# A hand-written queue order for four engines in the squared-ReLU MLP of a hybrid decoder layer

## The chip, the cores and the metric

The kernel runs on one core of one Trainium2 chip. The core has five engines that work side by side, each on its own queue of instructions: TensorE (PE in the profile, its weight loads PEld), VectorE (DVE), ScalarE (ACT), GpSimd (POOL) and SyncE (SP), which here only issues transfers. Transfers (DMA) from HBM are issued from the queues of SP and of POOL. The metric is the device time of one launch in microseconds, the median of several runs.

## The reference

One decoder layer on 512 tokens of width 1024, all in float32: an RMSNorm, an attention mixer with two head groups, an output projection with residual, then the part that this change touches, the MLP, and a final RMSNorm:

```python
def squared_relu_mlp(h, w_up, w_down):
    return jnp.square(jax.nn.relu(h @ w_up)) @ w_down
...
        h = h + squared_relu_mlp(rmsnorm(h, g_mlp[l]), w_up[l], w_down[l])
    return rmsnorm(h, g_final)
```

`w_up` is 1024 by 4096, `w_down` 4096 by 1024.

## The kernel before

**Precision.** Each float32 operand is split into a high part (rounded to the matmul type fp32r) and a low part, the rest. A product takes three matmuls, high by high, high by low and low by high (`mm3`, L189 to L192). A split is one ScalarE copy (`wh`, `sh`) and one VectorE subtract (`wl`, `sl`, recorded at L118, the helper `sub`). So each weight piece, 128 by 1024 values or 512 KB, costs a transfer, a copy and a subtract before TensorE can use it.

**The MLP in eight groups.** `for e in range(8)` (L1222) takes 512 of the 4096 hidden columns at a time. A group has four up pieces (`f` = 0 to 3, 24 matmuls each). After each, ScalarE does ReLU (L1237) and square (L1238) out of the PSUM bank, and the hidden values are split. The weights of the up pieces come through `ring` (L122 to L180): raw tile `wr` in two buffers, halves split at L164 (high) and L118 (low). Group 0 then does a plain down product: four pieces `wd`, 96 matmuls over four token blocks. Groups 1 to 7 use a scheme with seven products instead of eight (`product`, L1215, 12 matmuls each), in the order A11, S1, S2, A12, S3, S4, A22. Its inputs are sums of hidden blocks, made by `strassen_in` (L1192): R tiles on VectorE, copies at L1197, subtracts at L118. Its weights are sums of down pieces, built by transfers: `more` (L1125, L1127) adds a piece onto a loaded one by an accumulating transfer from POOL's queue, `down_piece` (L1117 to L1123) forms high and low parts mostly by transfers. One raw tile x serves four of the seven weights in turn: it is loaded, split (L1113, L1114), added to, split again, and so on; y serves one.

**PSUM.** Eight banks are handed out in a cycle by `nbank`. `evac` (L1153) adds a bank into the residual `h1`. The products S2, S3, S4 and A22 reuse the banks of earlier ones, so their first matmul waits until `evac` has read what stood there.

**The end.** In group 7, `norm_out` (L1157 to L1182) makes the final norm: a multiply by the gain `gfb` (L1164), a sum of squares on ScalarE (L1167), and for the last part of each token block Ln, Exp, three small VectorE operations, two scalings (L1181) and two transfers out. The last product, A22, is cut into three parts (L1297 to L1303), so that its pieces are finished one by one. The second and the third part share a PSUM bank.

**What sets the order.** TensorE's queue is always written by hand (L75). For the other four engines, the attention part is written by hand up to L1037 (`everything`). From there to the end the framework's scheduler decides in which order their instructions enter each queue. Each engine then runs its own queue strictly in order: an instruction that waits holds back all behind it.

Of the kernel before, what the change touches and what calls it, by code (L numbers as in the profile page):

```python
# [15 lines left out]
P = 128  # L16
D = 1024
S = 512
# [35 lines left out]
def hybrid_layer(tc, x, xT, wp, wfg, cst, gfin, out):  # L54
# [1022 lines left out]
    for tb in range(NT):  # L1077
# [9 lines left out]
        wout_evac(ps, tb, 1)  # L1087
    early = []
# [28 lines left out]
    def down_piece(i):  # L1117

        hi, lo = down_tiles()
        nc.gpsimd.dma_start(hi, wp[i])  # L1120
        nc.scalar.activation(lo, f32(hi), AF.Copy, scale=-1.0)
        nc.gpsimd.dma_start(lo, wp[i], accum_op=ALU.add)
        return [hi], [lo]  # L1123

    def more(r, i):  # L1125

        nc.gpsimd.dma_start(r, wp[i], accum_op=ALU.add)  # L1127

# [28 lines left out]
    def norm_out(tb, c, n, last):  # L1157
# [6 lines left out]
        nc.vector.tensor_tensor(o[:, c:c + n], h, gfb[:, c:c + n], op=ALU.mult)  # L1164
# [27 lines left out]
    def strassen_in(R, sh, sl, p, i):  # L1192
# [13 lines left out]
        sub(nc.vector, R[:, 4], R[:, 3], R[:, 1])  # L1206
        split(S1, 1)
        negsum(5, 0, 4)
        split(S2, 1)
        split(A12, 2)  # L1210
# [10 lines left out]

    for e in range(8):  # L1222
        sh = mp.tile([P, 2, 7, 256], F32R, tag="sh", name=nm("sh"))
        sl = mp.tile([P, 2, 7, 256], F32R, tag="sl", name=nm("sl"))
        ah, al = [t.rearrange("p a b c -> p (a b c)")[:, 0:4 * S].rearrange("p (f t) -> p f t", f=4) for t in (sh, sl)]
        for f in range(4):
            if early:
                w, ps = early.pop(0)
                up_mm(ps, w, range(4, NK))
            else:  # L1230
                w, ps = ring.piece(), nbank()
                up_mm(ps, w, range(NK))
            t = mp.tile([P, S], F32, tag="mt", name=nm("mt"), bufs=2)
            if f % 2 == 0:
                R = mp.tile([P, 8, 256], F32, tag="R", name=nm("R"), bufs=2)
            a = R[:, 2 * (f % 2):2 * (f % 2) + 2, :].rearrange("p a t -> p (a t)")
            nc.scalar.activation(t, ps, AF.Relu)  # L1237
            nc.scalar.activation(a, t, AF.Square)  # L1238
            if e > 0:
                strassen_in(R, sh, sl, f // 2, f % 2)  # L1240
            else:
                nc.scalar.activation(ah[:, f, :], a, AF.Copy)  # L1242
                sub(nc.vector, al[:, f, :], a, f32(ah[:, f, :]))
        w11, w12, w21, w22 = range(next_piece[0], next_piece[0] + 4)
        next_piece[0] += 4
        if e == 0:
            wd = [down_split(raw(i)) for i in (w11, w12, w21, w22)]
            for tb in range(NT):
                pss = [nbank() for _ in range(2)]
                tok = tokens(tb)  # L1250
                for fs in ((0, 1, 2), (3,)) if tb == 0 else ((0, 1, 2, 3),):
                    for half in range(2):
                        for f in fs:
                            mm3(pss[half], ah[:, f, tok], al[:, f, tok], *part(wd[f], 512 * half, 512), f == 0, f == 3)
                for half in range(2):
                    evac(pss[half], tb, 512 * half)
            continue
        pa, pd, pc = [[nbank() for _ in range(2)] for _ in range(3)]
        x, y = raw(w11), raw(w12)
        more(y, w22)  # L1260
        if e == 7:
            gfb = raw()
            nc.sync.dma_start(gfb, gfin.to_broadcast([P, D]))
        product(pa, A11, down_split(x), True, sh, sl)
        for k in range(2):
            evac(pa[k], k, 0)
        more(x, w12)
        product(pd, S1, down_split(x), True, sh, sl)
        for k in range(2):
            evac(pd[k], 2 + k, 512, True)  # L1270
        more(x, w22)
        product(pa, S2, down_split(x), False, sh, sl)
        for k in range(2):
            evac(pa[k], k, 512, True)
        product(pc, A12, down_piece(w21), True, sh, sl)
        for k in range(2):
            evac(pc[k], k, 0)
            if e == 7:
                norm_out(k, 0, 512, False)
# [131 lines left out]
```

## Time and profile before

| | us |
|---|---|
| median of 3 runs | 668.19 |
| lowest, highest | 667.58, 668.45 |
| the profiled execution | 667.41 |
| its span, first to last instruction | 665.6 |
| busy: PE, DVE, ACT, POOL | 637.7, 467.8, 365.5, 173.5 |

The span is shorter than the time by 1.81 us, which lie around it. Busy times are of an engine's instructions, not of its waiting; matmuls overlap, so a busy PE can still hold small gaps. The granted clock is the share of full speed that TensorE had.

### The profile page before, as it was taken

Reading aid. Unit: us, or ns where it says so; the run is one execution under the profiler, and the core shown is the slowest. Engines: PE = TensorE matmul, PEld = TensorE weight load, DVE = VectorE, ACT = ScalarE, POOL = GpSimd, SP = SyncE. Lnnn points to the kernel's source line nnn. Section 1 sums busy time; section 2 is a strip of 40 time slices with the busy share of each in tenths; the row PEclk is TensorE's granted clock in tenths of the full one; section 3 lists DMA queues with packets and bytes.
Section 4 is the critical chain, followed back from the end, with each engine's and each line's share of the span. In section 5 each row is a group of like instructions: output and inputs, shape, how many; then the busy total and the mean of one; then the engine's idle time right before and its main releaser. Section 6 shows DMA issues by size and latency. Waiting matters only on the chain.

```text
span 665.6 us, 9186 instructions
## 1 busy us (share of the span) xinstructions
PE 637.7 (96%) x3075; PEld 521.2 (78%) x3075; DVE 467.8 (70%) x1032; ACT 365.5 (55%) x776; POOL 173.5 (26%) x223
## 2 busy tenths in 40 slices
PE   9999999999999999999969999999999999999993
PEld 7867788878887878888848888788787887877882
DVE  5798887867866789948623575766756767567577
ACT  5435536777867878738612635617347173371633
POOL 0262062655756745200101102012021110101100
PEclk9999999999999999999969999999999999999997
DMA  8723621001122574134962935849569385572803
GB/s 273 235 95 127 213 72 33 2 33 32 33 82 71 127 219 109 53 105 176 284 141 54 245 109 136 248 90 245 151 134 266 80 242 154 130 184 35 187 1 126
DMA packets 28926, 88.74 MB, mean 133 GB/s; under 512 B 4944, under 2 KB 5584, under 8 KB 28880
## 3 DMA queue, kind: packets, MB, share of 16 engines
q1 hardware_dynamic: 20672, 58.76, 26.5%
q0 software_dynamic: 8064, 29.36, 21.6%
q8 instruction: 24, 0.39, 0.2%
q14 instruction: 22, 0.18, 0.1%
q10 hardware_dynamic: 144, 0.04, 0.0%
HBM read 81.83 MB, written 2.10 MB: 126 GB/s over the span
## 4 chain that ended last, share of the span: by engine, by line
PE 45%; DMA 22%; DVE 17%; ACT 9%; issue 5%; SPq 1%; POOL 1%; DVEq 0%; ACTq 0%; POOLq 0%
DMA wr<-wp_d 18%; DVE wl L118 5%; PE acc L190 4%; PE acc L191 4%; PE acc L192 4%; DVE h L1153 4%; PE O L756 4%; PE T L738 4%; PE S L192 3%; PE S L190 3%; PE S L191 3%; ACT wh L164 2%; ACT wh L1113 2%; PE S L710 2%; PE O L190 2%
## 5 line engine op out<-in xcount | busy, mean ns | idle before, releaser
L118 DVE TENSOR_TENSOR wl<-wr,wh 128x512 fp32r<-128x512 f32 (+1 forms) x141 | 123.1, 886 | 99.0 <-ACT wh L164 64.4
L164 ACT ACTIVATE wh<-wr 128x512 fp32r<-128x512 f32 x120 | 72.5, 623 | 61.0 <-DMA wr<-wp_d 26.5
L1113 ACT ACTIVATE wh<-wr 128x1024 fp32r<-128x1024 f32 x39 | 40.3, 1052 | 105.7 <-DMA wr<-wp_d 86.5
L1127 POOL DMA_DIRECT2D wr<-wp_d x28 | 24.5, 879 | 267.0 <-DVE wl L118 194.0
L720 ACT ACTIVATE sp<-sp,st 128x128 f32<-128x128 f32 (+1 forms) x96 | 53.2, 555 | 17.2 <-DVE st L718 16.6
L718 DVE CUSTOM_DVE_ANT_0 sp<-S,c 128x128 f32<-128x128 f32 (+1 forms) x96 | 43.1, 486 | 18.6 <-PE S L711 18.1
L726 POOL TENSOR_SCALAR sp<-sp,st,gt 128x128 f32<-128x128 f32 (+1 forms) x64 | 38.2, 607 | 47.8 <-ACT sp L720 26.9
L118 DVE TENSOR_TENSOR ptl<-T,pth 128x128 fp32r<-128x128 f32 (+1 forms) x96 | 44.3, 483 | 2.9 <-ACT pth L748 2.4
L748 ACT ACTIVATE pth<-T 128x128 fp32r<-128x128 f32 (+1 forms) x96 | 38.4, 426 | 9.8 <-PE T L738 9.2
L190 PE MATMUL S<-wh,sh 128*128 128x512 f32 (+1 forms) x92 | 36.2, 394 | 5.2 <-DVE h L1153 4.1
L738 PE MATMUL T<-c,sp 128*128 128x128 f32 x240 | 38.4, 274 | 2.5 <-DVE st L724 1.3
L118 DVE TENSOR_TENSOR sl<-R,sh 128x256 fp32r<-128x256 f32 (+1 forms) x74 | 37.7, 534 | 2.8 <-ACT sh L1242 1.7
L738 PEld LDWEIGHTS T<-c,sp 128*128 128x128 f32 x240 | 29.6, 140 | 12.4 <-issue 4.5
L1197 ACT ACTIVATE sh<-R 128x256 fp32r<-128x256 f32 (+1 forms) x70 | 33.8, 502 | 8.8 <-DVE R L1201 7.9
L191 PE MATMUL S<-wh,sl 128*128 128x512 f32 (+1 forms) x92 | 36.1, 392 | 0.0
L192 PE MATMUL S<-wl,sh 128*128 128x512 f32 (+1 forms) x92 | 35.9, 391 | 0.0
L190 PE MATMUL S<-uh,wh 128*128 128x512 f32 x88 | 34.4, 391 | 0.0
L191 PE MATMUL S<-uh,wl 128*128 128x512 f32 x88 | 34.3, 390 | 0.0
L192 PE MATMUL S<-ul,wh 128*128 128x512 f32 x88 | 34.3, 389 | 0.0
L190 PE MATMUL acc<-xh,wh 128*128 128x512 f32 x72 | 31.0, 430 | 0.0
L190 PE MATMUL T<-wh,sh 128*128 128x512 f32 x60 | 24.0, 401 | 6.2 <-ACT sh L1242 6.0
L192 PE MATMUL acc<-xl,wh 128*128 128x512 f32 x72 | 28.4, 395 | 0.0
(361 smaller groups left out, 1795.0 us busy)
## 6 DMA issues: line engine op xcount, KB each, us to landing
wr<-wp_d SPq DMA_DIRECT2D x77, 512.0 KB, 4.3
wr<-wp_d POOLq DMA_DIRECT2D x28, 512.0 KB, 5.5
wh<-wp_d POOLq DMA_DIRECT2D x14, 512.0 KB, 6.2
wl<-wp_d POOLq DMA_DIRECT2D x14, 512.0 KB, 9.2
wx<-wp_d SPq DMA_DIRECT2D x10, 512.0 KB, 4.3
xr<-x_d SPq DMA_DIRECT2D x4, 512.0 KB, 7.9
out_d<-wr SPq DMA_DIRECT2D x8, 256.0 KB, 2.2
xr<-xT_d SPq DMA_DIRECT2D x3, 512.0 KB, 6.6
```

The lines of the kernel that those rows point to most:

```text
L118: eng.tensor_tensor(o, a, b, op=ALU.subtract)
L164: high = lambda: nc.scalar.activation(hi, raw[:, c], AF.Copy)
L190: nc.tensor.matmul(ps, lh, rh, start=first, stop=False, **kw)
L191: nc.tensor.matmul(ps, ll, rh, start=False, stop=False, **kw)
L192: nc.tensor.matmul(ps, lh, rl, start=False, stop=last, **kw)
L718: nc.vector.tensor_tensor_reduce(out=self.p[i], in0=self.ps[i], in1=self.bias(i), scale=1.0, scalar=1e35, op0=ALU.add, op1=ALU.min, accum_ ...
L720: nc.scalar.activation(self.p[i], self.p[i], AF.Exp, bias=m, scale=-1.0, accum_out=den)
L726: nc.gpsimd.tensor_scalar(self.p[i], self.p[i], rs, g, op0=ALU.mult, op1=ALU.mult)
L738: nc.tensor.transpose(pt[:, j * P:j * P + P], self.p[i][:, j * P:j * P + P], ident)
L748: nc.scalar.activation(self.blocks(self.th, i), self.pt[i], AF.Copy)
L1113: nc.scalar.activation(hi, r, AF.Copy)
L1197: nc.scalar.activation(sh[:, p, o], r, AF.Copy)
```

## The change

The MLP from L1129 on gets an order of its own for VectorE, ScalarE, GpSimd and SyncE: the program text is rearranged, and a second `manual_schedule` block makes each of the four queues follow it. The set of operations stays the same but for one: the multiply by `gfb` goes from VectorE to GpSimd, except in the last quarter row.

- Up pieces: `up_fetch(g)` issues the load, `up_split(g)` the split, two steps ahead of the matmuls that use the piece, and after a split the load of the piece two further on.
- Group 0: the loads of its four down pieces, then of up pieces 3 and 4, stand first in SP's queue; each down piece is split in the step of its number. x and y of group 1 are loaded after the last up piece of group 0, and x is split between the second and third token block.
- Groups 1 to 7: the weight splits for S1, S3 and S2 stand before the matmuls of f = 1, 2 and 3, that for A22 behind the evacuation of S2, that for the next group's A11 behind the evacuation of A12.
- `hidden` does ReLU, square and the splits. For f = 3 the splits of A12, S3 and S4 are held back (a generator) until the evacuation of A11 is in the queue.
- The last group's `norm_out` calls stand where they stood in the text, and now bind.

```diff
+    first_up = next_piece[0]
...
-    def down_piece(i):
+    def down_whole(i):
         hi, lo = down_tiles()
         nc.gpsimd.dma_start(hi, wp[i])
+        yield [hi], [lo]
         nc.scalar.activation(lo, f32(hi), AF.Copy, scale=-1.0)
         nc.gpsimd.dma_start(lo, wp[i], accum_op=ALU.add)
-        return [hi], [lo]
+        yield
...
+    def up_fetch(g):
+        if g < 32:
+            up_raws[g] = rp.tile([P, 1024], F32, tag="wr", name=nm("wr"), bufs=2)
+            nc.sync.dma_start(up_raws[g], wp[piece_at(g // 4, g % 4)])
+
+    def up_split(g):
+        if not 2 < g < 32:
+            return
+        r, w = up_raws.pop(g), ([], [])
+        for k in range(2):
+            c = slice(512 * k, 512 * k + 512)
+            hi = rp.tile([P, 512], F32R, tag="wh", name=nm("wh"), bufs=6)
+            lo = rp.tile([P, 512], F32R, tag="wl", name=nm("wl"), bufs=6)
+            nc.scalar.activation(hi, r[:, c], AF.Copy)
+            sub(nc.vector, lo, r[:, c], f32(hi))
...
+        up_fetch(g + 2)
+
+    everything = tc.manual_schedule(engines={mybir.EngineType.DVE, mybir.EngineType.Activation, mybir.EngineType.Pool,
+                                               mybir.EngineType.SP})
+    everything.__enter__()
...
-        nc.vector.tensor_tensor(o[:, c:c + n], h, gfb[:, c:c + n], op=ALU.mult)
+        (nc.vector if tb == 3 and last else nc.gpsimd).tensor_tensor(o[:, c:c + n], h, gfb[:, c:c + n], op=ALU.mult)
...
         sub(nc.vector, R[:, 4], R[:, 3], R[:, 1])
+        negsum(5, 0, 4)
         split(S1, 1)
-        negsum(5, 0, 4)
         split(S2, 1)
+        yield
         split(A12, 2)
...
+    def hidden(e, f, ps):
...
+        nc.scalar.activation(t, ps, AF.Relu)
+        nc.scalar.activation(a, t, AF.Square)
+        if e > 0:
+            rest = strassen_in(R, cur["sh"], cur["sl"], f // 2, f % 2)
+            next(rest, None)
+            return rest
...
+    def load_sums(e):
+        X[e], Y[e] = raw(piece_at(e, 4)), raw(piece_at(e, 5))
+
+    def first_sum(e):
+        T[e, 1] = down_split(X[e])
+        more(X[e], piece_at(e, 5))
+        more(Y[e], piece_at(e, 7))
+
+    def next_sum(e, n, i):
+        T[e, n] = down_split(X[e])
+        if i is not None:
+            more(X[e], piece_at(e, i))
+
+    def whole(e, n, i):
+        g = down_whole(piece_at(e, i))
+        T[e, n] = next(g)
+        return g
+
+    downs = [raw(piece_at(0, 4 + i)) for i in range(4)]
+    up_fetch(3)
+    up_fetch(4)
...
     for e in range(8):
...
         for f in range(4):
+            if e == 0:
+                T[0, f] = down_split(downs[f])
+            elif f == 0:
+                if e == 1:
+                    wholes[1, 2] = whole(1, 2, 6)
+                wholes[e, 3] = whole(e, 3, 7)
+            elif f == 1:
+                next_sum(e, 5, 7)
+                next(wholes[e, 2])
+            elif f == 2:
+                T[e, 7] = down_split(Y[e])
+                next(wholes[e, 3])
+            else:
+                next_sum(e, 6, 6)
+            up_split(4 * e + f + 2)
...
+            rest = hidden(e, f, ps)
+            if f < 3:
+                next(rest, None)
         if e == 0:
+            load_sums(1)
             for tb in range(NT):
+                if tb == 2:
+                    first_sum(1)
...
         pa, pd, pc = [[nbank() for _ in range(2)] for _ in range(3)]
+        if e < 7:
+            load_sums(e + 1)
...
+        product(pa, A11, T[e, 1], True, sh, sl)
+        both(pa, 0, 0)
+        next(rest, None)
+        product(pd, S1, T[e, 5], True, sh, sl)
+        both(pd, 2, 512, True)
+        product(pa, S2, T[e, 6], False, sh, sl)
+        both(pa, 0, 512, True)
+        next_sum(e, 4, None)
+        product(pc, A12, T[e, 2], True, sh, sl)
+        both(pc, 0, 0)
+        if e < 7:
+            first_sum(e + 1)
+        else:
+            for k in range(2):
+                norm_out(k, 0, 512, False)
+        product(pa, S3, T[e, 7], False, sh, sl)
+        both(pa, 2, 512, True)
+        if e == 7:
+            for k in range(2):
+                norm_out(2 + k, 512, 512, False)
+        product(pd, S4, T[e, 3], False, sh, sl)
+        both(pd, 0, 512, True)
+        if e < 7:
+            wholes[e + 1, 2] = whole(e + 1, 2, 6)
+            product(pa, A22, T[e, 4], False, sh, sl)
+            both(pa, 2, 0)
+            continue
         for k in range(2):
...
+            norm_out(k, 512, 512, True)
         for k, c, n in ((0, 0, 512), (1, 0, 256), (1, 256, 256)):
...
             evac(pa[k][:, c:c + n], 2 + k, c, n=n)
             norm_out(2 + k, c, n, c + n == 512)
+    everything.__exit__(None, None, None)
```

`both` is `evac` for the two banks of a product, `T` holds the finished weights, `X` and `Y` are the raw tiles x and y by group.

## Rows read from the trace of the kernel before

**Rows 1.** The page's first part: busy microseconds, share of the span and instructions of each engine.

```profile
PE 637.7 (96%) x3075; PEld 521.2 (78%) x3075; DVE 467.8 (70%) x1032; ACT 365.5 (55%) x776; POOL 173.5 (26%) x223
```

**Rows 2.** What TensorE waited for from 300 us on: matmul's tile and line, the releaser; total us, times, longest.

```profile
PE T L190 <- ACT sh L1242: 6.0, 1, 6.0
PE S L190 <- DVE h L1153: 4.1, 1, 4.1
```

**Rows 3.** Busy time by stage: the down product of group 0 with its waits, groups 1 to 6 (from the first up matmul of a group to that of the next), the rest from A22's first matmul on; then a stretch inside the first row. Columns: from:to, length, busy (instructions) of PE, PEld, DVE, ACT and POOL, granted clock, DMA share, GB/s.

```profile
330.56:361.78 31.22, 25.18 (x97) 19.95 (x96) 8.75 (x11) 4.98 (x7) 1.42 (x2) 0.84 0.43 94
361.78:402.65 40.87, 40.87 (x181) 33.80 (x180) 26.37 (x44) 18.77 (x32) 4.89 (x6) 1.00 0.66 168
402.65:444.25 41.60, 41.44 (x181) 33.64 (x180) 27.61 (x46) 20.09 (x33) 6.27 (x8) 1.00 0.70 177
444.25:486.71 42.46, 41.76 (x181) 33.63 (x180) 28.07 (x46) 20.08 (x33) 6.29 (x8) 1.00 0.70 174
486.71:528.26 41.55, 41.42 (x182) 33.63 (x180) 27.99 (x46) 20.08 (x33) 6.29 (x8) 1.00 0.69 177
528.26:571.19 42.93, 41.73 (x181) 33.63 (x180) 27.87 (x46) 20.09 (x33) 6.33 (x8) 1.00 0.67 172
571.19:613.18 41.99, 41.77 (x182) 33.62 (x180) 27.93 (x46) 19.97 (x33) 5.44 (x7) 1.00 0.54 125
651.32:665.60 14.28, 3.77 (x19) 3.03 (x17) 10.28 (x31) 4.91 (x18) 0.00 (x0) 0.73 0.40 147
...
340.90:347.30 6.40, 6.40 (x15) 4.76 (x16) 2.14 (x3) 0.00 (x0) 0.15 (x1) 0.51 0.84 164
```

**Rows 4.** The chain of waits through the gap in group 0: start, us, what.

```profile
324.75 12.80 DMA wr<-wp_d
...
337.57 1.06 ACT wh L1113
...
340.87 0.80 PE T L190
```

**Rows 5.** Group 5 in order of time, ScalarE and TensorE: start, us, instruction, in brackets the idle time before it and its releaser.

```profile
552.11 0.63 ACT L164 ACTIVATE wh<-wr 128x512 fp32r<-128x512 f32 x1 [4.74 <-DMA wr<-wp_d]
552.65 0.58 ACT L1237 ACTIVATE mt<-O 128x512 f32<-128x512 f32 x1
...
555.31 0.51 PE L190 MATMUL S<-wh,sh 128*128 128x512 f32 x1 [0.99 <-ACT sh L1197]
```

**Rows 6.** Single instructions in order of time, for durations: ScalarE, then VectorE.

```profile
307.02 1.14 ACT L164 ACTIVATE wh<-wr 128x512 fp32r<-128x512 f32 x2
...
408.38 2.01 ACT L1113 ACTIVATE wh<-wr 128x1024 fp32r<-128x1024 f32 x2 [2.15 <-DMA wr<-wp_d]
...
635.17 0.60 ACT L1237 ACTIVATE mt<-O 128x512 f32<-128x512 f32 x1 [3.73 <-PE O L192]
635.80 0.63 ACT L1238 ACTIVATE R<-mt 128x512 f32<-128x512 f32 x1
...
636.46 0.42 DVE L118 TENSOR_TENSOR R<-R 128x256 f32<-128x256 f32 x1 [4.57 <-ACT R L1238]
636.92 0.43 DVE L1201 SCALAR_TENSOR_TENSOR R<-R 128x256 f32<-128x256 f32 x1
637.26 1.36 DVE L118 TENSOR_TENSOR sl<-R,sh 128x512 fp32r<-128x512 f32 x3
```

**Rows 7.** Transfers of 512 KB by kind from 362 to 613 us (out<-in, queue, count, KB each, median us from issue to landing), then two single ones, issued at 421.88 (accumulating) and at 458.41 (a load).

```profile
wr<-wp_d SPq DMA_DIRECT2D x32, 512.0 KB, 5.9
wr<-wp_d POOLq DMA_DIRECT2D x22, 512.0 KB, 5.5
wl<-wp_d POOLq DMA_DIRECT2D x12, 512.0 KB, 9.4
...
wr<-wp_d POOLq DMA_DIRECT2D x1, 512.0 KB, 8.3
...
wr<-wp_d SPq DMA_DIRECT2D x1, 512.0 KB, 9.1
```

**Rows 8.** The end, VectorE and ScalarE in order of time.

```profile
650.84 0.75 DVE L1153 SCALAR_TENSOR_TENSOR h<-acc,n2s,h 128x512 f32<-128x512 f32 x1
651.68 0.63 ACT L1167 ACTIVATE jo<-h 128x512 f32<-128x512 f32 x1 [1.32 <-DVE h L1153]
652.44 0.29 ACT L1174 ACTIVATE t<-sso,eb 128x1 f32<-128x1 f32 x1
...
657.09 0.47 DVE L1153 SCALAR_TENSOR_TENSOR h<-S,r2s,h 128x256 f32<-128x256 f32 x1
...
660.26 0.29 ACT L1174 ACTIVATE t<-sso,eb 128x1 f32<-128x1 f32 x1
661.27 1.00 DVE L1181 TENSOR_SCALAR wr<-wr,r,t 128x512 f32<-128x512 f32 x2
```

**Rows 9.** GpSimd's two-input operation: first its group in the list by line and shape (busy us, mean ns), then single instructions of GpSimd and VectorE in order of time.

```profile
L118 POOL TENSOR_TENSOR wl<-wr,wh 128x512 fp32r<-128x512 f32 x18 | 24.5, 1381 | 3.5 <-ACT wh L164 3.4
...
28.54 1.43 POOL L531 TENSOR_TENSOR ck<-ck,r 128x512 f32<-128x512 f32 x1 [7.56 <-DVE r L205]
28.38 2.14 DVE L118 TENSOR_TENSOR wl<-wr,wh 128x512 fp32r<-128x512 f32 x2
31.05 1.28 DVE L118 TENSOR_TENSOR wl<-wx,wh 128x512 fp32r<-128x512 f32 x2
```

More of the change, by code (lines that the diff above doesn't have):

```diff
@@ new lines, in hybrid_layer @@
+    cur, X, Y, T = {}, {}, {}, {}
+    def load_sums(e):
[13 more added lines that the diff above has]
+    downs = [raw(piece_at(0, 4 + i)) for i in range(4)]
@@ L1222, in hybrid_layer @@
+    up_fetch(3)
+    up_fetch(4)
+    wholes = {}
     for e in range(8):
[L1223 to L1225 removed]
+        for n in ("sh", "sl"):
+            cur[n] = mp.tile([P, 2, 7, 256], F32R, tag=n, name=nm(n))
+        sh, sl = cur["sh"], cur["sl"]
         for f in range(4):
[L1227 removed]
+            if e == 0:
[13 more added lines that the diff above has]
+            up_split(4 * e + f + 2)
+            if e == 0 and f < 3:
@@ L1230, in hybrid_layer @@
             else:
[L1231 to L1245, printed above, removed]
+                ps = nbank()
+                up_mm(ps, up_ready.pop(4 * e + f), range(NK))
+            rest = hidden(e, f, ps)
+            if f < 3:
+                next(rest, None)
         if e == 0:
-            wd = [down_split(raw(i)) for i in (w11, w12, w21, w22)]
+            ah, al = cur["a"]
+            load_sums(1)
             for tb in range(NT):
+                if tb == 2:
+                    first_sum(1)
                 pss = [nbank() for _ in range(2)]
@@ L1257, in hybrid_layer, with both @@
             continue
+        def both(banks, tb, c, neg=False):
+            for k in range(2):
+                evac(banks[k], tb + k, c, neg)
         pa, pd, pc = [[nbank() for _ in range(2)] for _ in range(3)]
-        x, y = raw(w11), raw(w12)
-        more(y, w22)
-        if e == 7:
+        if e < 7:
+            load_sums(e + 1)
+        else:
             gfb = raw()
             nc.sync.dma_start(gfb, gfin.to_broadcast([P, D]))
-        product(pa, A11, down_split(x), True, sh, sl)
@@ L1265, in hybrid_layer @@
-        for k in range(2):
[L1266 to L1279, printed above, removed]
@@ L1280, in hybrid_layer @@
-        product(pa, S3, down_split(y), False, sh, sl)
-        for k in range(2):
-            evac(pa[k], 2 + k, 512, True)
-            if e == 7:
-                norm_out(2 + k, 512, 512, False)
-        product(pd, S4, down_piece(w22), False, sh, sl)
-        for k in range(2):
-            evac(pd[k], k, 512, True)
-            if e == 7:
-                norm_out(k, 512, 512, True)
-        more(x, w21)
-        w = down_split(x)
-        if e < 7:
-            product(pa, A22, w, False, sh, sl)
-            for k in range(2):
-                evac(pa[k], 2 + k, 0)
-            continue
+        product(pa, A11, T[e, 1], True, sh, sl)
```

25 lines of the change are left out of this document (22 added, 3 removed).

## Prediction, made before the changed kernel ran

> **What bounds the kernel now.** I began with the busy shares: TensorE is busy for 637.7 of 665.6 us [rows 1], so the kernel is bound by matmuls. What another order can win is time in which TensorE stands still or runs slowly. The list of its waits names two long ones in the MLP, 6.0 us on ScalarE and 4.1 us on VectorE [rows 2]. The table by stage says what they cost [rows 3]. Group 1 takes 40.87 us for its 180 matmuls with TensorE busy throughout: 0.227 us per matmul, the floor. Groups 2 to 6 take 41.60, 42.46, 41.55, 42.93 and 41.99, together 6.18 us over five floors. The down product of group 0 takes 31.22 us for 96 matmuls, whose floor is 96 x 0.227 = 21.8: 9.4 us over. The last 14.28 us hold 3.77 us of matmuls: an end in which a chain of small operations rules.
>
> Then the reasons. In group 0 the chain of waits [rows 4] shows TensorE waiting for ScalarE, whose weight copy (L1113) had waited for a sum of weights of group 1 that took 12.80 us to land. The ReLU of group 0's last up piece stood behind that copy in the queue. So work for the next group held up work needed at once. After the gap the granted clock is 0.51 for 6.40 us, the lower level, 1.2 GHz, and 15 matmuls run at about half speed [rows 3]; this is part of the 9.4. In group 5 it is the same in small: ScalarE idles 4.74 us for the load of an up piece, copies it, and only then does the ReLU, and TensorE then waits 0.99 us for a copy of S1 or S2 [rows 5].
>
> **Durations.** ScalarE: a half up piece 0.52 us (two end 1.14 after the first starts), a down piece 0.96, ReLU to square 0.63, square to the next operation 0.66. VectorE: a 256-wide operation 0.42, one that depends on it 0.46 later, three subtracts in a row 1.36 [rows 6]; an evacuation 0.75 [rows 8].
>
> **Group 0 in the new order.** Per up piece ScalarE has ReLU, square and copy (0.63 + 0.66 + 0.53), the next down piece (0.96) and two up halves (1.04): 3.82 us. From the end of f = 0 the matmuls of f = 1, 2 and 3 need 12 + 12 + 24 matmuls, 10.9 us; three such steps are 11.5, so the last ReLU comes 0.6 us late. Its split takes 0.63 + 0.66 + 0.63 + 0.68 = 2.6, ready 3.2 us after the matmuls of f = 3. TensorE meanwhile has 18 matmuls over f = 0 to 2, 4.1 us: no wait, 0.9 to spare. Up piece 3 is split 3.82 + 0.68 = 4.5 us after f = 0 and wanted at 5.4. Nothing of group 1 stands in front any more: x and y are loaded behind the last up piece. So the whole 9.4 us should go, the slow clock with it.
>
> **Groups 1 to 6.** Here the order must carry itself. The worst step is f = 2: ScalarE still has the chain of f = 1 (up to the S3 copy about 4.9 us: 1.29 to the square's end, 0.91 to the first subtract, 1.3 for three, 0.8 for R6 and R7, 0.52), then two down pieces (1.92) and two halves (1.04): 7.9 us against 5.44 of matmuls. In f = 3 it has 1.6 + 0.96 + 1.04, reaching the last ReLU at 11.5 against 10.9: 0.6 late. S1 is then ready 0.63 + 0.66 + 0.46 + 0.46 + 0.42 = 2.6 after that ReLU's start, some 3.4 us after A11 begins, and is wanted at 18 matmuls, 4.1. The two evacuations of A11 come next on VectorE and end at about 4.8 and 5.4; S2 wants the first bank at 5.4 and the second at 6.1. So about 0.6 us to spare at both places, and no stall: 6.2 us gained. The splits of up pieces, ahead of the ReLU before too, no longer wait, because a load is issued two steps, some 10.5 us, before its split; single loads took 5.9 at the median, 9.1 in a burst [rows 7]. The held-back splits of f = 3 (A12, S3, S4) fall into 8 us of A11, S1 and S2.
>
> **The end.** Here the order written down costs. Let T be the time since A11 of group 7 began (before: 72 matmuls ahead of A22, which began at 651.32 [rows 3], so at 651.32 - 72 x 0.227 = 634.98; S4's first evacuation at 650.84 [rows 8] is T 15.9). VectorE must now finish both last `norm_out` calls before the first evacuation of A22. Each needs its multiply from GpSimd, 1.38 us [rows 9]; four multiplies queue from T 11.7 (when A12 is evacuated) and the two last follow at once: done at 11.7 + 5 x 1.38 = 18.6 and 20.0. Ln to scaling is 1.01 us, squares to Ln 0.76 [rows 8]; the first scaling could start at T 18.6. Whether VectorE may scale while GpSimd multiplies is a price that no row shows for this very operation. From below: no hindrance, then the second pair of scalings runs at T 20.0 to 21.0. From above: the nearest row. A pair of two-input subtracts took 2.14 us while a GpSimd operation of 1.43 us ran, 1.28 without one [rows 9]: VectorE stood until GpSimd was done. Then the first pair starts at 20.0 and the second ends at 22.3. I take this, since the scaling too works from tile to tile in SBUF. A22's first part is then evacuated, and its own `norm_out` (0.77 + 0.76 + 1.01 to the scaling, 0.92 for it, some 3.5 with the evacuation's start) delays the second evacuation to T 25.7; without hindrance 24.4. Before, it began at 657.09, T 22.1 [rows 8]. From there on nothing changes. So the end is 3.6 us longer; with the lower bound 2.3.
>
> The Trainium skill, SBUF — State Buffer, SBUF: two separate sides, says that VectorE and GpSimd share one pair of ports, held exclusively for a whole instruction when VectorE works in a two-port mode or with two SBUF inputs, and it so speaks against moving the multiply. The trace agrees for two inputs (2.14 against 1.28); for the scaling no run here shows it yet. By the rule the sum is the one with 3.6, without it 1.3 us less.
>
> **Sum.** Profiled execution 667.41 - 9.4 - 6.2 + 3.6 = 655.4; the median of the runs is 0.8 above that execution, so 656.2. I say 656.0. A measurement of this kernel can tell about 0.2%, 1.3 us, from no change.
>
> **Rivals.**
> - *Stalls stay in the groups.* The 0.6 us to spare is thin: a load or sum landing a microsecond late (needed 10.5 to 11 us after issue, 8.3 to 9.4 seen [rows 7]) or a ReLU late by more sends the rest to TensorE, 0.5 to 1 us in each of six groups: 3 to 6 us, 659 to 662. For it: the old order lost as much. Against: the lengths above fit.
> - *Group 0 still waits* (the change doesn't do there what it says): the schedule between L1037 and L1129 is still the framework's, and if it puts the start of the new block 2 us late, TensorE waits for f = 3 and may lose its clock again: up to 9 us, 660 to 665.
> - *The x sums set the pace* (the other side). Each group's x is loaded, split and added to three times in a row, at fixed places in the queues. The last sum is issued about 1.2 us after A11 begins; its copy, low half, two evacuations, the next group's low half and one evacuation (1.1 + 1.2 + 1.3 + 1.2 + 0.8 = 5.6) must be done when A22 begins at 16.3. So it must land within 9.5 us. Sums now take 5.5 at the median, 8.3 at worst in these groups, but the low halves, behind others, 9.4 [rows 7]. From 9.5 on, each microsecond costs about one in each of six groups; at 11.7 the gain of 12.0 is eaten, beyond it the kernel is slower than before, 670 at 12.
> - *The end is not longer*: no hindrance, and multiplies shorter than 1.38: 653 to 654.5.
>
> **Chances.** The forecast with its two bounds (654.5 to 658) 0.60; stalls stay 0.17; group 0 waits 0.08; the end not longer 0.05; x sums 0.06, of which 0.05 slower; nothing moves (the gains lost one way or another) 0.04. Faster: 0.60 + 0.17 + 0.08 + 0.05 + 0.01 = 0.91; same 0.04; slower 0.05. The range 653 to 662 holds the first two, nearly all of the fourth and a quarter of the third: about 0.83.
>
> **What the new profile would show.** Right: no TensorE wait in the MLP but the one of its last matmuls; clock 1.00 throughout group 0; groups of 40.9 us; L1164's successor on POOL at about 1.4 us each; the second A22 evacuation 25 to 26 us after A11 of group 7 begins; the list of TensorE's waits with one entry of 6 to 8 us, the last part of A22. Wrong: `sh` or `h` in TensorE's waits for several groups, or ScalarE idle for `wr` at f = 3 or before the A22 weights.

## The result, and the profile after

The changed kernel took 655.93 us at the median of four runs (655.69 to 656.97), the kernel before 667.88 beside it (667.25 to 668.45): a ratio of 0.9824, 95% interval 0.9807 to 0.9841. The profiled execution took 655.86 us with a span of 654.1. The forecast was 656.0.

The busy shares of the changed kernel (us, share of the span, instructions):

```profile
PE 630.2 (96%) x3075; PEld 519.6 (79%) x3075; DVE 470.0 (72%) x1024; ACT 368.5 (56%) x776; POOL 183.9 (28%) x231
```

TensorE lost 7.5 us of busy time [rows 1] although it does the same matmuls. By the stages, 3.4 of it went in group 0's down product (25.18 to 21.79), where matmuls had run at half speed, and 3.8 in groups 2 to 6 (208.1 to 204.3), where the clock was 1.00 before and after: there small gaps between overlapping matmuls had counted as busy. TensorE's list of waits from 310 us to the end has one entry (total, times, longest):

```profile
PE S L190 <- DVE h L1185: 7.8, 1, 7.8
```

It is the last part of A22, in the end. Of the two long entries of before [rows 2] only the first, 6.0 us, is gone. The second, 4.1 us, was this same wait (it ended at 657.62, where A22's last part began), and it has grown to 7.8. The table by stage (us; PE, PEld, DVE, ACT, POOL busy; granted clock, DMA share, GB/s): the down product of group 0, groups 1 to 6, and the end from A22 on.

```profile
330.75:352.54 21.79, 21.79 (x98) 18.02 (x96) 9.31 (x12) 4.75 (x8) 3.07 (x4) 1.00 0.57 159
352.54:393.41 40.87, 40.87 (x182) 33.78 (x181) 28.38 (x45) 20.54 (x33) 6.39 (x8) 1.00 0.65 157
393.41:434.27 40.86, 40.86 (x181) 33.78 (x180) 28.57 (x46) 20.54 (x33) 6.37 (x8) 1.00 0.73 181
434.27:475.14 40.87, 40.87 (x182) 33.78 (x180) 28.58 (x46) 20.43 (x33) 6.37 (x8) 1.00 0.73 181
475.14:516.01 40.87, 40.87 (x182) 33.79 (x181) 28.56 (x46) 20.54 (x33) 6.35 (x8) 1.00 0.71 175
516.01:556.87 40.86, 40.86 (x181) 33.78 (x180) 28.55 (x46) 20.54 (x33) 6.37 (x8) 1.00 0.75 182
556.87:597.74 40.87, 40.87 (x182) 33.78 (x180) 28.57 (x46) 20.43 (x33) 6.36 (x8) 1.00 0.77 197
...
635.87:654.10 18.23, 3.89 (x19) 3.15 (x17) 11.02 (x27) 5.07 (x18) 4.99 (x5) 0.68 0.31 115
```

Set against [rows 3]: group 0's down product 31.22 to 21.79, with the clock at 1.00, is -9.43. Groups 2 to 6 now stand at the floor of 40.87: -6.18. The end, from the start of A11 of group 7 (619.53) to the last instruction, is 34.57 against 665.60 - 634.97 = 30.63: +3.94. The MLP's down product began 0.19 later than before (330.75 against 330.56). The sum is -11.5, and the spans differ by 654.1 - 665.6 = -11.5. Nothing is left over.

The end in order of time, VectorE first, then GpSimd (start, us, instruction; T is the time less 619.53):

```profile
634.36 0.15 DVE L1201 TENSOR_SCALAR eb<-sso 128x1 f32<-128x1 f32 x1 [0.19 <-ACT jo L1199]
...
636.08 0.75 DVE L1185 SCALAR_TENSOR_TENSOR h<-O,n2s,h 128x512 f32<-128x512 f32 x1
637.00 0.64 DVE L1208 SCALAR_TENSOR_TENSOR v<-sso,eb 128x1 f32<-128x1 f32 x1 [0.17 <-ACT jo L1199]
637.75 1.13 DVE L1209 SCALAR_TENSOR_TENSOR t<-r,v 128x1 f32<-128x1 f32 x1
...
639.17 1.00 DVE L1213 TENSOR_SCALAR wr<-wr,r,t 128x512 f32<-128x512 f32 x2
640.09 0.15 DVE L1208 SCALAR_TENSOR_TENSOR v<-sso,eb 128x1 f32<-128x1 f32 x1
640.35 0.22 DVE L1209 SCALAR_TENSOR_TENSOR t<-r,v 128x1 f32<-128x1 f32 x1
...
640.79 1.00 DVE L1213 TENSOR_SCALAR wr<-wr,r,t 128x512 f32<-128x512 f32 x2
641.71 0.74 DVE L1185 SCALAR_TENSOR_TENSOR h<-T,r2s,h 128x512 f32<-128x512 f32 x1
...
645.35 0.48 DVE L1185 SCALAR_TENSOR_TENSOR h<-S,r2s,h 128x256 f32<-128x256 f32 x1
...
631.31 7.55 POOL L1196 TENSOR_TENSOR wr<-h,wr 128x512 f32<-128x512 f32 x6 [10.39 <-DVE h L1185]
```

Six multiplies run back to back on GpSimd until 638.86. While they run, two VectorE operations on a single column, v and t, take 0.64 and 1.13 us; after them the same two take 0.15 and 0.22. At 1.26 us for each multiply the fifth ends at 637.60 and the sixth at 638.86; v ends at 637.64 and t at 638.88. The evacuation at 636.08 and the one-column operation eb at 634.36, which has one input in SBUF, ran beside the multiplies at their usual 0.75 and 0.15. The evacuation of A22's first bank starts at T 22.2, that of the second at T 25.8, where before it started at T 22.1 [rows 8].

### The profile page after: what moved, and what is told of

Read it like the earlier page. It is cut to its first block, busy times and chain, and to the rows that moved or that the text cites. A ratio compares the mean times of both kernels' runs of the same rounds, so it can differ in the third digit from the quotient of the medians.

```text
span 654.1 us, 9165 instructions
## 1 busy us (share of the span) xinstructions
PE 630.2 (96%) x3075; PEld 519.6 (79%) x3075; DVE 470.0 (72%) x1024; ACT 368.5 (56%) x776; POOL 183.9 (28%) x231
## 4 chain that ended last, share of the span: by engine, by line
PE 84%; DVE 9%; DMA 2%; issue 2%; ACT 2%; SPq 0%; POOL 0%; DVEq 0%; ACTq 0%
PE S L192 8%; PE S L190 8%; PE S L191 8%; PE acc L190 6%; PE acc L192 6%; PE acc L191 6%; PE O L190 5%; PE O L192 5%; PE O L191 5%; PE T L192 5%; PE T L190 5%; PE T L191 5%; PE O L756 4%; PE T L738 4%; PE S L710 2%
## 5 line engine op out<-in xcount | busy, mean ns | idle before, releaser
L118 DVE TENSOR_TENSOR wl<-wr,wh 128x512 fp32r<-128x512 f32 (+1 forms) x141 | 120.2, 884 | 22.3 <-ACT wh L1114 11.4
L1129 POOL DMA_DIRECT2D wr<-wp_d x28 | 24.6, 959 | 246.4 <-DVE wl L118 246.4
L118 DVE TENSOR_TENSOR sl<-R,sh 128x256 fp32r<-128x256 f32 (+1 forms) x74 | 39.9, 539 | 60.3 <-ACT sh L1229 52.8
L164 ACT ACTIVATE wh<-wr 128x512 fp32r<-128x512 f32 x62 | 36.3, 622 | 15.3 <-DMA wr<-wp_d 7.1
L1150 ACT ACTIVATE wh<-wr 128x512 fp32r<-128x512 f32 x58 | 32.9, 615 | 0.0
L1262 ACT ACTIVATE mt<-S 128x512 f32<-128x512 f32 x11 | 6.4, 585 | 39.9 <-PE S L192 39.9
```

The source lines that it names most:

```text
L118: eng.tensor_tensor(o, a, b, op=ALU.subtract)
L164: high = lambda: nc.scalar.activation(hi, raw[:, c], AF.Copy)
```

## Experiments

Beside the three groups of runs that follow, the kernel before took 665.97, 667.20 and 665.94 us. Small differences are therefore read from stages of the profiles, not from times on different chips.

### Which part of the change wins what

My theory was that the hand order is the cause of both gains. Four kernels divide it.

**Hand order for group 0 alone.**

```diff
         if e == 0:
...
                 for half in range(2):
                     evac(pss[half], tb, 512 * half)
+            everything.__exit__(None, None, None)
             continue
...
-    everything.__exit__(None, None, None)
```

> The new text, but the hand-written order of the four engines ends after group 0; groups 1 to 7 and the end are ordered by the scheduler again. If the three terms are separate, the 9.4 us of group 0 are gained, the groups keep stalls of some 6 us and the end is as long as before: about 658.5 (667.9 - 9.4). Rival: the rearranged text alone, which the scheduler takes as its priorities, already removes the stalls of the groups: about 652.

Measured: 659.55 us (656.91 to 662.29), ratio 0.9899 (0.9859 to 0.9938). The table by stage: group 0's down product, groups 1 and 2, and the end from A11 of group 7 on.

```profile
330.92:352.71 21.79, 21.79 (x97) 18.02 (x96) 10.83 (x15) 5.95 (x10) 3.21 (x4) 1.00 0.81 246
352.71:396.36 43.65, 41.48 (x182) 33.71 (x180) 27.02 (x44) 19.32 (x33) 6.31 (x8) 1.00 0.78 187
396.36:439.04 42.68, 41.45 (x182) 33.71 (x180) 27.89 (x45) 19.70 (x34) 6.34 (x8) 1.00 0.69 173
...
627.68:657.60 29.92, 19.55 (x91) 16.08 (x89) 21.94 (x49) 11.76 (x33) 9.56 (x8) 0.87 0.19 70
```

Group 0 is cured, the groups stall again (8.0 us over six floors, where the kernel before lost 6.2), and the end is 29.92, shorter than by hand (34.57) by 4.65. The time lies 1 us above the 658.5 expected: the stalls were 1.8 larger than in the kernel before, the end 0.7 shorter.

**Hand order for the groups alone.** The first kernel for this moved only the block's entry. In its trace ScalarE goes through group 0 in the changed kernel's order all the same, so the order seems to be taken from where the block is created, and the run is a repeat of the changed kernel.

```diff
-    everything.__enter__()
...
+            everything.__enter__()
             continue
```

> The other half: the scheduler orders group 0, the hand-written order begins with group 1. If it is the scheduler's queue order that put work of group 1 in front of group 0's last ReLU, the 9.4 us come back: about 665. Rival: the loads of x and y now stand behind group 0's last up piece in the text, and that alone cures it: about 656.

Measured: 655.77 us (655.49 to 656.07), ratio 0.9842 (0.9816 to 0.9867), a second measurement of the change. It decides nothing between the theory and the rival, though the rival's number came out. The next kernel also creates the block there, at the end of group 0's branch:

```diff
-    everything = tc.manual_schedule(engines={mybir.EngineType.DVE, mybir.EngineType.Activation, mybir.EngineType.Pool,
-                                               mybir.EngineType.SP})
-    everything.__enter__()
...
+            everything = tc.manual_schedule(engines={mybir.EngineType.DVE, mybir.EngineType.Activation, mybir.EngineType.Pool,
+                                                       mybir.EngineType.SP})
+            everything.__enter__()
             continue
```

> The scheduler orders group 0 and the hand order opens only at the end of group 0's branch, so groups 1 to 6 and the end are in the hand order. My theory (the scheduler's order puts group 1's work ahead of group 0's last ReLU, and the hand order of group 0 is what takes that away): here nothing of group 1 is in the scheduled stretch, so the scheduler has nothing to put ahead; group 0's down projection then lasts 21.8 us without a long wait, the groups 40.9 each and the time is that of the changed kernel, 655.5 to 656.5. Rival (the scheduler's order is bad for group 0 by itself, whatever is behind it): down of group 0 stays near 31 us and the time is 664 to 666.

Measured: 656.1 us (655.39 to 656.41), ratio 0.9826 (0.9805 to 0.9847). Group 0's down product and group 1, in the order of the scheduler and by hand:

```profile
330.66:352.46 21.80, 21.80 (x98) 18.02 (x96) 6.57 (x9) 2.27 (x4) 0.56 (x1) 1.00 0.16 56
352.46:393.32 40.86, 40.86 (x181) 33.78 (x180) 27.18 (x43) 20.54 (x33) 6.38 (x8) 1.00 0.55 137
```

Group 0 needs no hand order when nothing of group 1 is there to be put in front.

**The rearranged text, no hand order at all.**

```diff
-    everything = tc.manual_schedule(engines={mybir.EngineType.DVE, mybir.EngineType.Activation, mybir.EngineType.Pool,
-                                               mybir.EngineType.SP})
-    everything.__enter__()
...
-    everything.__exit__(None, None, None)
```

> The text of the changed kernel, its statements in their new order, but no hand-written block in the MLP: the scheduler orders the four engines, with the text's order as its priorities. My theory (the scheduler's model of times, not the order of the statements, makes it issue work of the next group ahead): group 0's wait returns in part or whole, the groups stall by 1 to 2 us each as in the kernel before, and the time is 663 to 668. Rival A (the order of the text was the cure): 655.5 to 656.5, groups 40.9. Rival B (the text cures group 0 alone, the groups keep stalling): 659 to 661.

Measured: 656.78 us (654.86 to 658.24), ratio 0.9836 (0.9807 to 0.9864), a span of 655.7. My theory fell: group 0's wait did not return. Rival B had the mechanism and missed the time by 2.2 us at least; the end by the scheduler is 4.6 us shorter than by hand, which its sum did not have. Stages: group 0's down product, groups 1, 2 and 5, the end.

```profile
330.50:352.29 21.79, 21.79 (x98) 18.02 (x96) 6.88 (x10) 3.67 (x6) 1.42 (x2) 1.00 0.46 116
352.29:393.16 40.87, 40.87 (x182) 33.79 (x181) 27.20 (x44) 19.07 (x32) 6.33 (x8) 1.00 0.75 191
393.16:435.97 42.81, 41.60 (x182) 33.63 (x180) 27.89 (x45) 19.90 (x33) 6.33 (x8) 1.00 0.69 172
...
520.32:563.11 42.79, 41.85 (x182) 33.62 (x180) 27.89 (x45) 20.46 (x34) 6.41 (x8) 1.00 0.69 172
...
625.77:655.70 29.93, 19.55 (x91) 16.08 (x89) 21.94 (x49) 11.76 (x33) 9.56 (x8) 0.86 0.19 70
```

ScalarE at the last ReLU of group 0, then in group 5 the copy of an up piece and the last ReLU:

```profile
327.97 0.63 ACT L1150 ACTIVATE wh<-wr 128x512 fp32r<-128x512 f32 x1 [0.42 <-PE O L192]
330.69 0.60 ACT L1258 ACTIVATE mt<-O 128x512 f32<-128x512 f32 x1 [2.10 <-PE O L192]
...
540.37 0.63 ACT L1150 ACTIVATE wh<-wr 128x512 fp32r<-128x512 f32 x1 [4.77 <-DMA wr<-wp_d]
...
544.69 0.58 ACT L1258 ACTIVATE mt<-O 128x512 f32<-128x512 f32 x1
```

Here ScalarE idles 2.10 us and does the ReLU at 330.69; before, in the same place, it had taken up the copy that waited until 337.57 [rows 4].

In the groups the pattern is the one that the prediction read in [rows 5]: in group 5 ScalarE stands idle 4.77 us for the load of an up piece and only then goes on to its ReLUs. The last ReLU of groups 2 to 5 begins 2.60, 1.92, 2.01 and 2.58 us after the group's A11 (542.11 in group 5), in the kernel before 1.25, 2.13, 1.21 and 2.60. By hand it begins 0.96 after it, and no up piece is waited for there. That a late ReLU costs TensorE time is tested by itself below; whether the earlier loads or the place of the copies makes the ReLU early was not tried.

From A11 of group 7 on, this kernel's span differs from the changed one by +6.24 (625.77 against 619.53: the stalls of the groups, less 0.25 that its down product began earlier) and -4.64 (the end): 654.1 + 6.24 - 4.64 = 655.7. So in these two executions the hand order as such is worth 1.6 us of span: it wins the groups and pays most of it back in the end. The two stages differ by far more than 1.6, but as a time the 1.6 is not shown: the text-only kernel's four runs lie between 654.86 and 658.24, and the intervals of the two ratios overlap. The 9.4 us of group 0 came with the rearranged text; which of its changes turned the scheduler's order there was not tried.

### What group 0's loss was

One fault put back into the hand order: a copy that must wait for a sum, ahead of the last ReLU. For that x and y of group 1 are loaded earlier, and the copy of x itself comes ahead of the ReLU as well.

```diff
                 T[0, f] = down_split(downs[f])
+                if f == 2:
+                    load_sums(1)
+                elif f == 3:
+                    first_sum(1)
+                    next_sum(1, 5, 7)
...
             elif f == 1:
-                next_sum(e, 5, 7)
+                if e > 1:
+                    next_sum(e, 5, 7)
...
-            load_sums(1)
...
-                if tb == 2:
-                    first_sum(1)
```

> The changed kernel's hand order with one fault put back: x and y of group 1 are loaded in the step of f = 2 of group 0, and in the step of f = 3, ahead of the last ReLU, ScalarE copies x, a sum is added to it, and the copy of that sum stands ahead of the ReLU too, as in the kernel before. My theory (one copy that waits for a sum, ahead of a ReLU that is ready, is the whole of group 0's loss): x lands at 331 to 333, its sum 8 to 9 us later, the ReLU starts at 341 to 343 instead of 331, TensorE waits 8 to 11 us, its clock falls for a while, the down product of group 0 takes 32 to 36 us against 21.8, groups 1 to 6 stay at 40.9, and the time is 666 to 670. Rival (the wait lies in the loads or in group 0's own splits, not in the copy): down of group 0 stays under 25 us, time under 659.

Measured: 667.2 us (666.43 to 668.52), 1.0025 of the kernel before (1.001 to 1.004). ScalarE, then TensorE at the gap:

```profile
332.39 1.06 ACT L1114 ACTIVATE wh<-wr 128x1024 fp32r<-128x1024 f32 x1 [1.06 <-DMA wr<-wp_d]
340.46 1.06 ACT L1114 ACTIVATE wh<-wr 128x1024 fp32r<-128x1024 f32 x1 [7.01 <-DMA wr<-wp_d]
...
342.46 0.58 ACT L1262 ACTIVATE mt<-O 128x512 f32<-128x512 f32 x1
...
344.41 0.80 PE L190 MATMUL T<-wh,sh 128*128 128x512 f32 x1 [8.67 <-ACT sh L1270]
```

The stages: group 0's down product, group 1, and 7 us behind the gap.

```profile
331.48:365.02 33.54, 24.87 (x97) 19.76 (x96) 10.71 (x13) 5.94 (x9) 3.91 (x5) 0.85 0.38 90
365.02:405.89 40.87, 40.87 (x181) 33.78 (x180) 27.18 (x44) 19.59 (x32) 5.47 (x7) 1.00 0.59 153
...
345.00:352.00 7.00, 7.00 (x21) 5.52 (x21) 1.97 (x4) 0.40 (x1) 0.00 (x0) 0.64 0.56 140
```

The ReLU slips to 342.46, TensorE waits 8.67 us, and behind the wait the granted clock is 0.64 over 7 us in which only 21 matmuls run. The down product takes 33.54 instead of 21.79: 8.67 of waiting and about 3 of slow matmuls. The two copies in the wrong place, x and its sum, cost 11.75 us, and group 1 behind them is untouched. The kernel before had the sum's copy in this place, with the same pattern: copy at 337.57, ReLU at 338.54, TensorE waiting 6.04 us at the same matmul, and then a slow clock, 9.43 us together.

### How much the groups had to spare

**The last ReLU later.**

```diff
+        if e > 0 and f == 3:
+            for _ in range(3):
+                nc.scalar.activation(t, f32(uh[:, 0, :]), AF.Copy)
         nc.scalar.activation(t, ps, AF.Relu)
```

> Three ScalarE copies of 0.52 us, whose results are overwritten, stand ahead of the ReLU of f = 3 in groups 1 to 7: the ReLU is 1.57 us later. My theory (about 0.6 us to spare at S1, measured 0.4 to 0.6 in the changed kernel): TensorE stalls 1.0 to 1.2 us in each of the seven groups, groups 1 to 6 take 41.9 to 42.1 and the time is 663 to 664.5. Rival (more to spare than the durations say, since the ReLU also starts early when ScalarE idles ahead of it): groups below 41.3, time under 659.

Measured: 664.95 us (664.68 to 665.36). The three copies took 1.98 us, not 1.57 (459.93 to 461.91 on ScalarE in group 3). Groups 1 to 6 waited, each 0.89 us; group 7, where ScalarE has no up piece of a next group to split, did not. TensorE at S1 of group 3:

```profile
464.13 0.50 PE L190 MATMUL acc<-wh,sh 128*128 128x512 f32 x1 [0.89 <-ACT sh L1229]
464.59 0.50 PE L191 MATMUL acc<-wh,sl 128*128 128x512 f32 x1
464.92 0.40 PE L192 MATMUL acc<-wl,sh 128*128 128x512 f32 x1
465.15 0.39 PE L190 MATMUL O<-wh,sh 128*128 128x512 f32 x1
```

S1's second half, the one that needs f = 3, should begin 18 x 0.227 = 4.09 after A11 (458.97), at 463.06; it begins 1.07 later. A pad of 1.98 thus cost 1.07: some 0.9 us were to spare, where the prediction had 0.6. The group takes 42.31 instead of 40.87, so a wait of 0.89 costs 1.44: the first two matmuls behind it start 0.46 and 0.33 apart instead of 0.23, which is 0.33 more. The groups and the time lie above what I gave, for the longer pad and for these two matmuls.

**The third sum of x later.**

```diff
+    n2g = cp.tile([P, 4], F32, name="n2g")
...
-                next_sum(e, 6, 6)
+                next_sum(e, 6, None)
...
         both(pa, 0, 0)
         next(rest, None)
+        nc.gpsimd.tensor_tensor(n2g, h1[:, 1, 0:4], h1[:, 1, 0:4], op=ALU.add)
+        more(X[e], piece_at(e, 6))
```

> The third sum of x is issued only once the second bank of A11 is evacuated, at T 5.5 of its group instead of 1.6, by way of a GpSimd operation of 128x4 ahead of it that reads that bank's rows. It lands about 5.6 us later, at T 11.2. My theory (it must have landed by T 10.7 to 10.9): groups 1 to 6 lose 0.2 to 0.7 us each, 41.1 to 41.6, and the time is 657 to 660. Rival (the copy of the sum has more to spare, as other work stands in its way anyhow): groups stay at 40.9 and the time is within 0.6 us of the changed kernel's.

Measured: 677.9 us (two runs, 673.73 and 682.06), slower than before: ratio 1.0186 (1.0103 to 1.027). GpSimd's issue and ScalarE's copy in group 3, and TensorE's wait there:

```profile
470.43 0.87 POOL L1129 DMA_DIRECT2D wr<-wp_d  x1
476.32 2.01 ACT L1114 ACTIVATE wh<-wr 128x1024 fp32r<-128x1024 f32 x2 [4.62 <-DMA wr<-wp_d]
481.90 0.47 PE L190 MATMUL T<-wh,sh 128*128 128x512 f32 x1 [1.11 <-DVE h L1185]
```

Stretches behind waits, of groups 1, 2 and 3:

```profile
392.40:399.40 7.00, 7.00 (x24) 5.57 (x25) 4.53 (x7) 0.00 (x0) 2.38 (x4) 0.76 0.87 159
438.00:445.00 7.00, 6.95 (x24) 5.60 (x25) 4.51 (x7) 0.00 (x0) 2.41 (x4) 0.76 0.88 167
481.50:484.75 3.25, 2.85 (x13) 2.36 (x13) 2.71 (x5) 0.00 (x0) 2.76 (x4) 1.00 0.59 83
```

T is again the time since A11, here of the same group. In the four groups whose copy was released by the sum (1, 3, 4 and 6), the copy starts at T 12.84, 12.06, 13.62 and 14.49, and TensorE waits 1.88, 1.11, 2.68 and 3.54 for an evacuation. The differences are 10.94 to 10.96 each time: the sum must be there at T 10.95, and each microsecond behind that is one of waiting. I missed the time three times over. The sums were issued at T 6.2, not 5.5. They landed 6.7, 5.9, 7.4 and 8.3 us after their issue, where I had reckoned with 5.6. And waiting is not all that a group loses: with a wait of 1.11 it takes 42.30 (1.43 over the floor), with 2.68 it takes 45.18 (4.31 over). After the waits of 1.88 in group 1 and of 2.90 in group 2 the granted clock was 0.76 for 7 us, after 2.68 in group 4 as well; after 1.11 it stayed at 1.00.

### The end

**Does a GpSimd multiply hold a scaling up?** Two more multiplies, results unused, behind the others:

```diff
+        if last and tb == 1:
+            scr = mp.tile([P, 8, 256], F32, tag="R", name=nm("R"), bufs=2).rearrange("p a t -> p (a t)")
+            for q in range(2):
+                nc.gpsimd.tensor_tensor(scr[:, 512 * q:512 * q + 512], h, gfb[:, c:c + n], op=ALU.mult)
```

> Two more GpSimd multiplies of 128x512 behind the four of the end's first two token blocks; their results are not used. They keep GpSimd busy for 2.55 us longer, from T 19.4 to T 21.9 behind the last A11, while VectorE works on the norm of these blocks. If a GpSimd multiply holds every VectorE operation up, one-input scalings too: the first scaling comes 1 us or more late, the 128x1 additions of the second block are done no earlier than T 21.8, and the time is 1.5 to 2.5 us above the changed kernel. If it holds up only operations with two SBUF inputs, and scalings run free: the pair of scalings at T 19.6 keeps its 1.00 us for each, only the 128x1 operations stretch (0.64 and 1.13 in the changed kernel), and the time is 0 to 1.2 us above.

Measured: 658.15 us (657.63 and 658.67); the span is 655.9, 1.8 above the changed kernel.

```profile
637.91 1.13 DVE L1213 SCALAR_TENSOR_TENSOR t<-r,v 128x1 f32<-128x1 f32 x1
...
639.34 2.59 DVE L1217 TENSOR_SCALAR wr<-wr,r,t 128x512 f32<-128x512 f32 x2
...
642.55 1.00 DVE L1217 TENSOR_SCALAR wr<-wr,r,t 128x512 f32<-128x512 f32 x2
...
638.98 2.67 POOL L1200 TENSOR_TENSOR R<-h,wr 128x512 f32<-128x512 f32 x2
```

The pair of scalings beside the two multiplies takes 2.59 us, the next pair, without them, 1.00. So a one-input scaling is held up too.

**The multiplies back on VectorE.**

```diff
-        (nc.vector if tb == 3 and last else nc.gpsimd).tensor_tensor(o[:, c:c + n], h, gfb[:, c:c + n], op=ALU.mult)
+        nc.vector.tensor_tensor(o[:, c:c + n], h, gfb[:, c:c + n], op=ALU.mult)
```

> The changed kernel with the multiply by the final gain back on VectorE. In the changed kernel's trace VectorE's two-input operations of 128x1 waited 0.5 and 0.9 us for GpSimd's multiplies to end. If the hindrance costs, VectorE pays 0.6 us for each of the three multiplies in its last chain but waits for none of GpSimd's: the second evacuation of A22 comes some 0.8 us earlier, about 655.1. Rival: GpSimd's help is worth what it was meant to: 1 to 2 us slower.

Measured: 655.43 us (655.29 to 658.63), ratio 0.9848 (0.9814 to 0.9882), span 653.5. The second evacuation of A22 came at T 25.46, 0.36 us earlier than in the changed kernel, where I had expected 0.8. The move to GpSimd saved nothing: VectorE's 0.69 us for each multiply and its waits for GpSimd weigh about the same.

**A22's evacuations ahead of the last two `norm_out` calls.**

```diff
-        for k in range(2):
-            norm_out(k, 512, 512, True)
-        for k, c, n in ((0, 0, 512), (1, 0, 256), (1, 256, 256)):
+        def last_part(k, c, n):
...
-            norm_out(2 + k, c, n, c + n == 512)
+        last_part(0, 0, 512)
+        last_part(1, 0, 256)
+        norm_out(0, 512, 512, True)
+        last_part(1, 256, 256)
+        norm_out(1, 512, 512, True)
+        norm_out(2, 0, 512, True)
+        norm_out(3, 0, 256, False)
+        norm_out(3, 256, 256, True)
```

> The changed kernel with only the end reordered: the evacuations of A22's first two parts stand ahead of the last norm_out calls, the third behind the first call. If the 3.9 us that the end grew lie in the place of the evacuations in VectorE's queue, they come back and more, since TensorE's last part no longer waits 7.8 us: about 650 to 652. Rival: the end is bound by GpSimd's multiplies and the scalings, whatever the order: 654.5 or more.

Measured: 652.65 us (651.96 to 655.0), ratio 0.9803 (0.9766 to 0.984), span 650.9: 3.2 below the changed kernel's. TensorE's long wait shrinks from 7.8 to 0.6. The wait for GpSimd is still there, in t and in the first pair of scalings; all eight multiplies end at 640.80:

```profile
639.01 1.13 DVE L1209 SCALAR_TENSOR_TENSOR t<-r,v 128x1 f32<-128x1 f32 x1
...
640.44 1.11 DVE L1213 TENSOR_SCALAR wr<-wr,r,t 128x512 f32<-128x512 f32 x2
...
631.34 9.46 POOL L1196 TENSOR_TENSOR wr<-h,wr 128x512 f32<-128x512 f32 x8 [10.39 <-DVE h L1185]
```

**The same with two multiplies on VectorE.**

```diff
-        (nc.vector if tb == 3 and last else nc.gpsimd).tensor_tensor(o[:, c:c + n], h, gfb[:, c:c + n], op=ALU.mult)
+        (nc.vector if tb >= 2 and c < 512 else nc.gpsimd).tensor_tensor(o[:, c:c + n], h, gfb[:, c:c + n], op=ALU.mult)
```

> The end of the A22-first order, and the last multiplies by the gain split: those of the first 512 columns of the last two token blocks on VectorE (0.66 us each there against 1.28 on GpSimd), the others on GpSimd. My theory (behind the last evacuation only the norm of the last token block's own columns is left, and the GpSimd multiplies queued ahead of it delay it): the profiled span is 649 to 650.5 and the time about 651.5, some 1.2 us under the A22-first order alone (652.65). Rival (the multiplies on VectorE only move the delay to the evacuations): 652.5 to 654.

Measured: 652.53 us (652.38 to 652.61), ratio 0.9774 (0.975 to 0.9798), span 650.6. The expected 1.2 us did not come, the rival's time did; the span is 0.3 shorter than the last kernel's: t no longer waits (0.22 instead of 1.13), but VectorE spends 0.68 and 0.42 us on the two multiplies.

**The end left to the scheduler.**

```diff
         if e < 7:
             first_sum(e + 1)
         else:
+            everything.__exit__(None, None, None)
             for k in range(2):
                 norm_out(k, 0, 512, False)
...
-    everything.__exit__(None, None, None)
```

> The hand order up to the evacuation of A12 of group 7, and the scheduler for what follows. My theory (the two gains and the end are separate, and add): groups at 40.9 with the last A11 at 619.5, and the end as in the text-only kernel, 29.9 us instead of 34.6: a span of 649.3 to 650 and a time of 651 to 652. Rival (the scheduler starts anew in the middle of group 7 and loses there what it wins in the end, by late splits of A22's weights or by evacuations out of place): 653 to 656.

Measured: 651.84 us (651.73 to 652.56), ratio 0.9794 (0.9763 to 0.9825), span 650.8 in the profiled execution, the longest of the four. The groups keep 40.87 and the end takes 30.6. The gains add, as the theory had it; the last A11 came 0.66 later than in the changed kernel and the end was 0.7 longer than in the text-only one. All three ends beat the changed kernel by some 3 us of span; which of the three is best, their intervals don't tell.

## Why the prediction was right

**Group 0, -9.4.** Measured -9.43, and the reason holds: a copy that waits for a sum, put ahead of the ReLU, brings the loss back, slow clock included. What the prediction did not see is that this gain does not hang on the hand order: the rearranged text under the scheduler has it too.

**Groups 2 to 6, -6.2.** Measured -6.18. The list of TensorE's waits misled on one point: of its two long entries only the 6.0 lay in what the groups and group 0 could win; the 4.1 stood in the end. In group 3 of the changed kernel the last ReLU begins 0.96 us after A11 (the prediction: 0.6) and S1's low half is ready at T 3.72 (the prediction: 3.4, though its terms 0.6 and 2.6 add up to 3.2). The slack at S1 was all the same 0.9 us instead of 0.6, because the matmul that waits there needs only the high half, which comes earlier; the low half is used one matmul later. The slack at S2 was not measured by a run; in the trace the two evacuations of A11 end at T 4.84 and 5.50, against 4.8 and 5.4 predicted. The rival of the x sums was the sharpest number of the text: it asked for a landing within 9.5 us of an issue at T 1.2, so by T 10.7, and the runs show 10.95. The changed kernel came nearer to it than the medians of [rows 7] let one think: in group 4 the copy of the third sum waited for its transfer until 507.48, T 10.55 (A11 began at 496.93). There were 0.4 us left. The price that I gave beyond the limit, about one microsecond per microsecond, was too low: 1.43 for a wait of 1.11, and 4.31 for 2.68, behind which the clock fell. Even at the price given, the gain of 12.0 would have been eaten at 11.5, not at 11.7.

**The end, +3.6.** Measured +3.94. The second evacuation of A22 came at T 25.82 (25.7), which is +3.7 over before; some 0.2 more came in the small steps behind it. The size was right, partly by luck, and the way there was not. The multiplies took 7.55 / 6 = 1.26 us instead of 1.38, so the six were done at T 19.3 and not 20.0, and the scalings, at T 19.6 and 21.3, met no multiply. The hindrance fell on v and t ahead of them: 0.64 + 1.13 instead of 0.15 + 0.22, 1.4 us. I had taken the upper bound for the scalings; about as much was paid, by operations whose work is one column, for which I had reckoned nothing. That the second pair of scalings ended at T 22.26, where the upper bound put it (22.3), is two errors that offset each other: faster multiplies, and a hindrance elsewhere. That a scaling is held up as well, the open price of the text, is shown by the two extra multiplies: 2.59 against 1.00.

The Trainium skill, SBUF — State Buffer, SBUF: two separate sides, names both cases, two SBUF inputs and a two-port mode. The traces agree with the first: v and t have two SBUF inputs and waited for the multiply's end. A scaling has one SBUF input and was held up too; that it runs in a two-port mode no row shows. Evacuations, with one input in PSUM, kept 0.75 us beside the multiplies (636.08 in the changed kernel), as by the same rule.

**The rivals.** Stalls in the groups and a wait in group 0 did not come. The end was not shorter. The x sums did not set the pace, by 0.4 us in the nearest group.

**The sum and its parts.** The sum came out since the two gains were separate and exact, and with some luck in the rest: the profiled execution took 655.86 where the terms gave 655.4, and of the 0.8 added for the median almost nothing came (655.93). But the change was several things, and its hand order taken alone is worth 1.6 us of span in the profiled executions: 6.2 won in the groups against an end that is 4.6 longer than what the scheduler makes of the same text. The prediction compared the end to the end before (30.63), which hid that the scheduler would have had 29.9.

## What to carry to other kernels

Read a stall from the queue of the engine that is late: an instruction waiting for a transfer ahead of one that is ready costs what it waits beyond the slack (ScalarE stood 8.92 us in the kernel before, TensorE 6.04), and then more while the clock is low. Here an order written by hand was worth its place where work repeats and there is little to spare, and not in the end. Where a kernel ends in a chain of small operations, write down which result is waited for by TensorE and put that first, or leave the end to the scheduler. Test a change of two parts by leaving one out: here the text alone gave nearly all of the time that was won.

## What the runs showed of the hardware

- A VectorE operation on 128x1 elements with two SBUF inputs waited for a running GpSimd multiply of 1.26 us: 0.64 and 1.13 us instead of 0.15 and 0.22. One on 128x1 with one SBUF input did not (0.15 beside the multiplies).
- A one-input fp32 scaling of 128x512 waited as well (a pair 2.59 us against 1.00), an evacuation from PSUM did not (0.75 against 0.75).
- A wait of TensorE of 0.89 us left the clock at 1.00 but cost 1.44: the next two matmuls started 0.46 and 0.33 apart instead of 0.23. After 1.11 us it stayed at 1.00 too; after 1.88 and after 2.90 us the granted clock was 0.76 over the next 7 us, after 8.67 us 0.64.
- The same accumulating transfer of 512 KB, at the same place of its group (T 1.57), landed within 5.8 us of its issue in group 3 of the changed kernel (issued at 457.63, copied at 463.40 without a wait) and 9.0 us after it in group 4 (498.50, 507.48).
